# Hybrid attention and HGRN2 layer on one core: value products in one pass of split operands, branch products by mixer on four banks, small zero products at the start

## The chip, the cores and the metric

The kernel runs on one core of one Trainium2 chip. The metric is the device time of one execution in microseconds (us). The engines are TensorE (PE, with its weight loads as PEld), VectorE (DVE), ScalarE (ACT), GpSimd (POOL) and the queue engine SP, which issues most DMAs.

## What is computed

One decoder layer over 512 tokens of 1024 features. Two token mixers read one input projection; their outputs are projected, gated, added, projected again, and a layer norm follows the residual. Cut to what matters:

```python
h = x @ w_in + b_in                   # 5912 columns
# mixer A: 8 heads of 64 in 2 groups; three branches, gated per head
o_cmp = softmax(q k_c^T) v_c          # 31 compressed blocks
o_slc = softmax(q_r k_slc^T) v_slc    # causal (all blocks are chosen at this length)
o_win = softmax(q_r k_win^T) v_win    # causal, window of 512
o_a = (g0*o_cmp + g1*o_slc + g2*o_win) * silu(z_a)
# mixer B: HGRN2, 4 heads of 128, chunks of 64
o_b = rmsnorm(hgrn2(q_b, f_b, i_b)) * norm_g * silu(z_b)
y = sigmoid(gm_a) * (o_a @ w_branch_a) + sigmoid(gm_b) * (o_b @ w_branch_b)
out = layer_norm(2**0.25 * x + y @ w_out)
```

Everything is float32.

## The kernel before, in words

Large products run on split operands: `split2` (L140) writes a ScalarE cast to float32r, the high part, and a VectorE subtraction, the low part. A product of two split operands is three single-pass products (high by high, high by low, low by high). Products that are not split are FP32 products, which the trace shows as two records each.

The order of TensorE, and of its DMAs on SP, is the program's own. `proj` (L239) makes a tile of 128 columns of the input projection: 24 products of 128x512 into one bank of the pool `pa` (two banks). Weight tiles come three tiles ahead, and are split two tiles ahead (`load`, `split`, L186 to L196). Before every six of these products, `weave.tick` (L77) lets chains of small steps go on: mixer B (`hgrn`, L330), its norm (`hgrn_norm`, L408), compressed keys and values, rotary embedding, scores (`attn_scores`, L591) and values (`attn_values`, L633). A chain says by `yield` how many ticks it waits; most numbers are in the table `D` (L64). The other engines take their instructions in the order that the tile scheduler gives them.

`attn_scores` and `attn_values` go by units: a query tile of 128 rows (3, 2, 1, 0) and one branch, or both for tiles 1 and 0. Scores of four heads are made, exponentiated and scaled by gate over sum. `attn_values` then takes one block of 128 keys at a time: for each half `ab` of the heads it transposes four 128x128 tiles of probabilities into a bank of `pst` (two banks), ScalarE copies them (L661), and one FP32 product with the tile `vtok` adds 64 output rows to the bank `po`:

```python
T.matmul(po[64 * ab:64 * ab + 64], vts[j][:, 128 * brs[x] + 64 * ab:128 * brs[x] + 64 * ab + 64],
         pts[ab], start=False, stop=brs[x] == 1 and j == i)
```

Here `vts[j]` is `vtok[:, j]`, the values of 128 keys. The two products of a block are a pair. They are issued after the transposes of the next block, or, for the last block of a unit, two ticks later. The compressed branch starts `po` of each query tile with four FP32 products of 128x128 (`vcB`). ScalarE copies `po` to `asum` (L673); VectorE multiplies with silu(z_a) (L679) and `split2` makes `oa`.

At the start, two zero products (L149) stand ahead of the first real ones, which need the first tiles of x and of the weights. After the last gate tile, `weave.drain()` (L775) finishes the chains. Then, for each of eight column tiles m, 12 products of mixer B and 12 of mixer A go to two `pa` banks; VectorE multiplies each with its gate (L804), adds them (L806), and `split2` makes a piece of y. The output projection (from L821) takes banks of `pa`, `pss` and `pst`. All small tiles come from the pool `t2`, with 69 buffers of 512 columns.

Of the kernel before, what the change touches and what calls it, by code (L numbers as in the profile page):

```python
# [9 lines left out]
F32 = mybir.dt.float32  # L10
# [14 lines left out]
# column groups of w_in  # L25
# [4 lines left out]
# feature tiles after the four of f_b, and the order of the large products  # L30
# [11 lines left out]

def _columns(name):
# [15 lines left out]
# columns of the array of constants  # L59
# [33 lines left out]
def layer_kernel(ctx: ExitStack, tc: tile.TileContext, xT, xn, w0, wi, wg, wf, small, brow, consts,  # L93
# [18 lines left out]
    t2 = ctx.enter_context(tc.tile_pool(name="t2", bufs=69))  # L112
# [23 lines left out]

    def act_set(name):
        return tc.keep_in_program_order(A.preload_act_table_set(name)).ins
# [5 lines left out]
    # ---- start: x, the gates and the four tiles of f_b, one contraction tile at a time  # L144
    A.preload_act_table_set("sigmoid_and_others")
# [11 lines left out]
    for kt in range(KT):  # L157
        xr, wr = T2(), T2()
        dma(xr, xT[:, kt])
        dma(wr, w0[kt])  # L160
# [22 lines left out]
    order = M_TILES + ["br%d" % m for m in range(8)]  # L183
# [38 lines left out]
    vtok = cst.tile([P, 4, 256], F32, name="vtok")  # L222
# [86 lines left out]
    # ---- HGRN2, in steps of two chunks  # L309
# [98 lines left out]
    def hgrn_norm():  # L408
# [20 lines left out]
        for h in range(4):  # L429
# [3 lines left out]
            V.tensor_tensor(o, o, rms[h], ALU.mult)  # L433
            yield 1
# [5 lines left out]
    # ---- compressed keys and values  # L440
# [75 lines left out]
    # ---- rotary embedding and exact two-part operands  # L516
# [36 lines left out]
    # ---- compressed branch: gated probabilities of two tiles' heads, transposed  # L553
# [33 lines left out]
    # ---- selected and window branches, by units of one query tile and one branch (or both)  # L587
# [45 lines left out]
    def attn_values():  # L633
        po = None
        for u, (i, brs) in enumerate(units):
            n, last = 128 * (i + 1), None
            while (u, 1) not in probs or len(PTc) < 2 or len(vts) < 4:
                yield 1
            if brs[0] == 0:
                po = PO()  # L640
                for m in range(4):
                    T.matmul(po[:, 128 * m:128 * m + 128], vcB[:, m], PTc[m // 2][:, 128 * i:128 * i + 128],
                             start=m == 0, stop=False)
                yield D["a1"]

            def products():
                x, j, pts = last
                for ab in range(2):
                    T.matmul(po[64 * ab:64 * ab + 64], vts[j][:, 128 * brs[x] + 64 * ab:128 * brs[x] + 64 * ab + 64],
                             pts[ab], start=False, stop=brs[x] == 1 and j == i)  # L650

            for x in range(len(brs)):
                for j in range(i + 1):
                    pts = []
                    for ab in range(2):
# [4 lines left out]
                        t = T2()  # L660
                        A.copy(t, ps)  # L661
# [10 lines left out]
            if brs[-1] == 1:  # L672
                A.copy(asum[:, :, 128 * i:128 * i + 128], po.rearrange("p (m q) -> p m q", m=4))  # L673
# [12 lines left out]
    # ---- the sequence of large products, the rest woven in  # L686
# [79 lines left out]
    # ---- merge gates: tanh of the half argument  # L766
# [8 lines left out]
    weave.drain()  # L775

    # ---- branch projections and merge; w_out is split alongside
# [9 lines left out]
    y = []  # L787
    load_out(0)
    for m in range(8):
        i = len(M_TILES) + m  # L790
        load(i + 3)
        split(i + 2)
        load_out(m + 1)
        hi, lo = parts[i]
        pp = []
        for s_, o4 in ((1, ob), (0, oa)):
            ps = PA()
            for kt in range(4):
                c = slice(128 * (4 * s_ + kt), 128 * (4 * s_ + kt) + 128)
                T.matmul(ps, hi[:, c], o4[kt][0], start=kt == 0, stop=False)  # L800
                T.matmul(ps, hi[:, c], o4[kt][1], start=False, stop=False)
                T.matmul(ps, lo[:, c], o4[kt][0], start=False, stop=kt == 3)
            r = T2()
            V.scalar_tensor_tensor(r, gm["g%s%d" % ("ab"[s_], m)], 1.0, ps, ALU.add, ALU.mult)  # L804
            pp.append(r)
        V.tensor_tensor(pp[0], pp[0], pp[1], ALU.add)  # L806
        hl = T2(dt=F32R), T2(dt=F32R)
        split2(pp[0], *hl)
        y.append(hl)
        hl = []  # L810
        for hf in range(2):
            hi, lo = T2(dt=F32R), T2(dt=F32R)
            split2(woraw[m][hf], hi, lo)
# [7 lines left out]
    # ---- output projection, residual, layer norm  # L821
# [118 lines left out]
```

## Time and profile before

| | before |
|---|---|
| time, median of 3 runs | 450.17 us (449.98 to 450.28) |
| profiled execution, span from its first to its last instruction | 450.8 us (no other time of its own is listed) |
| TensorE busy | 440.7 us, 98%, 2227 products |
| VectorE busy | 269.2 us, 60% |
| ScalarE busy | 223.3 us, 50% |
| GpSimd busy | 3.3 us |
| TensorE's mean granted clock | 0.996 |
| DMA queues | 47.38 MB, mean 105 GB/s |

Busy time of TensorE includes the pipeline, so that successive matmuls overlap in it: what a product costs is read from the starts of successive products, not from their durations. A row of a time line merges like instructions that follow each other (x4), with the time from the first start to the last end.

### The profile page before, as it was taken

What the parts mean: (1) busy time and instruction counts of PE and PEld (TensorE: products, weight loads), DVE (VectorE), ACT (ScalarE), POOL (GpSimd) and SP (SyncE); (2) the same over time, 40 slices, a digit from 0 to 9 for tenths busy, and PEclk for the clock granted to TensorE, in tenths of its full rate; (3) what the DMA queues carried; (4) which work ended last, traced back from release to release, by engine and by line L of the source; (5) the groups of instructions that cost most, each with busy time, mean ns of one, the idle gap of its engine ahead of it and who ended that gap; (6) DMA issues with size and microseconds to landing.
All of it is one profiled execution on the core that took longest, in us unless ns stands there. A gap on an engine that the chain in (4) does not pass through costs nothing.

```text
span 450.8 us, 6002 instructions
## 1 busy us (share of the span) xinstructions
PE 440.7 (98%) x2227; PEld 351.3 (78%) x2227; DVE 269.2 (60%) x550; ACT 223.3 (50%) x430; POOL 3.3 (1%) x16
## 2 busy tenths in 40 slices
PE   8999999999999999999999999999999999999993
PEld 5778888888898888888767687768767788878883
DVE  5905579994896479966433343445421688865554
ACT  3416543531547254687766556678854345344000
POOL 2000000000000000000000000000000000000000
PEclk9999999999999999999999999999999999999998
DMA  8982700222240544212111122111322452162111
GB/s 271 395 334 79 258 1 0 59 84 70 72 141 23 171 156 160 87 59 95 47 48 47 47 75 67 49 47 48 93 75 113 127 185 110 48 229 84 60 47 47
DMA packets 20444, 47.38 MB, mean 105 GB/s; under 512 B 2880, under 2 KB 3904, under 8 KB 20416
## 3 DMA queue, kind: packets, MB, share of 16 engines
q1 hardware_dynamic: 20416, 47.01, 31.3%
q8 instruction: 17, 0.28, 0.2%
q14 instruction: 11, 0.09, 0.1%
HBM read 41.76 MB, written 2.10 MB: 97 GB/s over the span
## 4 chain that ended last, share of the span: by engine, by line
PE 96%; DVE 2%; DMA 1%; issue 0%; DVEq 0%; SPq 0%
PE pa L101 66%; PE pss L101 15%; PE pso L101 10%; PE pst L105 4%; PE pst L101 1%; DMA t<-in_w_dram 1%; DVE t L455 0%; DVE wlo L142 0%; DVE t L856 0%; DVE t L858 0%; DVE t L804 0%; DVEq L936 0%; DVE t L353 0%; DVE sm_bst L848 0%; DVE t L169 0%
## 5 line engine op out<-in xcount | busy, mean ns | idle before, releaser
L101 PE MATMUL pa<-t,whi 128*128 128x512 f32 x704 | 223.7, 399 | 0.0
L101 PEld LDWEIGHTS pa<-t,whi 128*128 128x128 f32 x704 | 127.3, 188 | 38.2 <-issue 15.0
L101 PE MATMUL pa<-t,wlo 128*128 128x512 f32 x352 | 137.7, 391 | 0.0
L101 PEld LDWEIGHTS pa<-t,wlo 128*128 128x128 f32 x352 | 66.1, 188 | 14.6
L142 DVE TENSOR_TENSOR wlo<-wraw,whi 128x1024 fp32r<-128x1024 f32 x46 | 56.0, 1224 | 28.5 <-ACT whi L141 28.3
L141 ACT CAST whi<-wraw 128x1024 fp32r<-128x1024 f32 x46 | 48.2, 1049 | 42.8 <-PE pa L101 25.6
L614 DVE CUSTOM_DVE_ANT_0 t<-pss,t 128x512 f32<-128x512 f32 (+3 forms) x64 | 30.4, 489 | 58.6 <-PE pss L101 58.4
L101 PE MATMUL pss<-t,t 128*128 128x512 f32 (+5 forms) x296 | 49.4, 321 | 0.4 <-DVE t L361 0.4
L101 PEld LDWEIGHTS pss<-t,t 128*128 128x128 f32 (+1 forms) x296 | 39.2, 175 | 7.2 <-issue 0.7
L101 PE MATMUL pa<-t,t 128*128 128x512 f32 x192 | 44.6, 390 | 0.1
L617 ACT ACTIVATE t<-t,sm_mn 128x512 f32<-128x512 f32 (+3 forms) x64 | 35.8, 561 | 13.4 <-DVE sm_mn L614 13.1
L101 PEld LDWEIGHTS pa<-t,t 128*128 128x128 f32 x192 | 35.9, 188 | 7.9 <-DVE t L804 0.5
L661 ACT COPY t<-pst 128x512 f32<-128x512 f32 x40 | 23.3, 582 | 22.0 <-PE pst L105 21.7
L142 DVE TENSOR_TENSOR t<-t,t 128x512 fp32r<-128x512 f32 x36 | 23.0, 686 | 15.7 <-ACT t L141 15.7
L141 ACT CAST t<-t 128x512 fp32r<-128x512 f32 x36 | 20.4, 622 | 17.9 <-DVE t L806 14.4
L105 PE MATMUL pst<-con,t 128*128 128x128 f32 x185 | 28.1, 273 | 0.0
L105 PEld LDWEIGHTS pst<-con,t 128*128 128x128 f32 x185 | 22.7, 140 | 5.6 <-issue 1.6
L101 PE MATMUL pso<-t,t 128*128 128x128 f32 (+1 forms) x104 | 23.3, 344 | 0.7 <-DVE t L169 0.7
L101 PE MATMUL pso<-t,vtok 128*64 128x512 f32 x80 | 21.6, 618 | 0.0
L101 PEld LDWEIGHTS pso<-t,t 128*128 128x128 f32 x104 | 16.5, 198 | 4.8 <-ACT t L168 1.6
L628 ACT ACTIVATE t<-t,sm_dn 128x512 f32<-128x512 f32 (+3 forms) x32 | 16.3, 559 | 3.6 <-DVE sm_dn L623 3.6
L853 ACT ACTIVATE sm_rs<-sm_ag,epst 128x1 f32<-128x1 f32 x4 | 1.2, 296 | 33.3 <-DVE sm_ag L850 33.3
(144 smaller groups left out, 409.2 us busy)
## 6 DMA issues: line engine op xcount, KB each, us to landing
wraw<-in_wf_dram SPq DMA_DIRECT2D x38, 512.0 KB, 3.5
t<-in_w_dram SPq DMA_DIRECT2D x16, 256.0 KB, 5.9
wraw<-in_wbr_dram SPq DMA_DIRECT2D x8, 512.0 KB, 3.6
t<-in_wout_dram SPq DMA_DIRECT2D x16, 256.0 KB, 3.9
t<-t SPq DMA_DIRECT2D x48, 64.0 KB, 2.0
t<-in_xT_dram SPq DMA_DIRECT2D x8, 256.0 KB, 5.2
t<-in_wi_dram SPq DMA_DIRECT2D x8, 256.0 KB, 7.0
t<-in_xn_dram SPq DMA_DIRECT2D x8, 256.0 KB, 7.5
```

Of the source, the lines that this page charges most:

```text
L101: return tc.keep_in_program_order(nc.tensor.matmul(*a, **k))
L105: return tc.keep_in_program_order(nc.tensor.transpose(*a, **k))
L141: A.copy(dst_hi, src)
L142: V.tensor_tensor(dst_lo, src, dst_hi.bitcast(F32), ALU.subtract)
L614: V.tensor_tensor_reduce(out=p[:, c], in0=ps[:, c], in1=amask[:, 512 - n:512], op0=ALU.add, op1=ALU.min, scale=-0.125, scalar=3.0e38, accu ...
L617: A.activation(p[:, c], p[:, c], AF.Exp, bias=mn[:, k], scale=-1.0, accum_out=den[:, k])
L628: A.mul(ts[m][:, c], ts[m][:, c], den[:, k])
L661: A.copy(t, ps)
L853: A.activation(rs[:, 0:1], ag[:, 1:2], AF.Ln, bias=epst)
```

## The change

- Values: `v` is split into `vv`, in which a block holds, for each branch, 64 columns of high parts of one group, 128 of low parts and 64 of high parts of the other. `vv[..., 0:128]` is then high and low of group 0, and `[128:256]` low and high of group 1. The transposed probabilities are split by `split2` from PSUM. A pair becomes four products of 128x512 with float32r operands into two banks, one for each `ab`; high and low rows are added by VectorE afterwards, and GpSimd adds the sum to `asum`.
- Compressed values: four FP32 products of 128x512, one for each m, ahead of the units, copied to `asum` by ScalarE.
- Branch products: the weight tiles hold two column tiles of one mixer each, in the order `BRANCH` (b0 b2 a0 b4 a2 b6 a4 a6); the products go to `pa` and `pss` in turn, and the chains go on ticking between them, with the drain ahead of a0.
- Start: nine zero products of 128x128, and the first weights are loaded on ScalarE's queue.
- The norm's first product on GpSimd, six numbers in `D`, and 67 instead of 69 buffers in `t2`.

```diff
-D = dict(h0=9, h2=1, h3=6, h4=2, h5=8, h6=2, n0=5, n1=2, n2=10, c0=1, c1=6, c2=7, c3=7,
-         r0=5, p0=6, p1=13, a0=1, a1=3, a2=1, a3=1, a4=1, a5=1, s0=14, s1=21, s2=0, s3=2)
+D = dict(h0=8, h2=4, h3=6, h4=2, h5=8, h6=5, n0=3, n1=2, n2=10, c0=1, c1=6, c2=7, c3=7,
+         r0=5, p0=5, p1=13, a0=1, a1=3, a2=1, a3=1, a4=1, a5=1, s0=14, s1=21, s2=0, s3=2)
...
-    zero = T2()
+    first = T2(), T2()
+    dma_act(first[1], w0[0])
+    act_set("sigmoid_and_others")
+    zero = T2(128)
     V.memset(zero, 0.0)
     warm = PO()
-    for n in (512, 320):
-        T.matmul(warm[:, 0:n], zero[:, 0:128], zero[:, 0:n], start=True, stop=True)
+    for _ in range(9):
+        T.matmul(warm[:, 0:128], zero, zero, start=True, stop=True)
...
-            V.tensor_tensor(vtok[:, tt], ps[:, 0:256], brv, ALU.add)
-            vts.append(vtok[:, tt])
+            v = T2(256)
+            tc.keep_in_program_order(V.tensor_tensor(v, ps[:, 0:256], brv, ALU.add))
+            vd = vv[:, tt].rearrange("p b (g c) -> p b g c", c=64)
+            v4 = v.rearrange("p (b g c) -> p b g c", b=2, c=64)
+            split2(v4, vd[:, :, 0:4:3], vd[:, :, 1:3])
+            vts.append(vv[:, tt])
...
-            V.tensor_tensor(o, o, rms[h], ALU.mult)
-            yield 1
+            G.tensor_tensor(o, o, rms[h], ALU.mult)
+            yield 2
...
     def attn_values():
-        po = None
+        while len(PTc) < 2:
+            yield 1
+        for m in range(4):
+            po = PO()
+            T.matmul(po, vcB[:, m], PTc[m // 2], start=True, stop=True)
+            A.copy(asum[:, m], po)
+            yield 1
...
-                    T.matmul(po[64 * ab:64 * ab + 64], vts[j][:, 128 * brs[x] + 64 * ab:128 * brs[x] + 64 * ab + 64],
-                             pts[ab], start=False, stop=brs[x] == 1 and j == i)
+                    v = vts[j][:, brs[x], 128 * ab:128 * ab + 128]
+                    for k in range(2):
+                        T.matmul(acc[ab], v, pts[ab][k], start=brs[x] == 0 and j == 0 and k == 0,
+                                 stop=brs[x] == 1 and j == i and k == 1)
...
-                        t = T2()
-                        A.copy(t, ps)
+                        t = T2(dt=F32R), T2(dt=F32R)
+                        split2(ps, *t)
...
-                A.copy(asum[:, :, 128 * i:128 * i + 128], po.rearrange("p (m q) -> p m q", m=4))
+                o = T2()
+                for ab in range(2):
+                    own, other = slice(64 * ab, 64 * ab + 64), slice(64 - 64 * ab, 128 - 64 * ab)
+                    A.copy(o[own], acc[ab][other])
+                    V.tensor_tensor(o[own], o[own], acc[ab][own], ALU.add)
+                dst = asum[:, :, 128 * i:128 * i + 128]
+                G.tensor_tensor(dst, dst, o.rearrange("p (m q) -> p m q", m=4), ALU.add)
...
-    weave.drain()
...
+        if mix == "a" and m0 == 0:
+            weave.drain()
+        for m in (m0, m0 + 1):
+            ps = (PA, PS)[m % 2]()
             for kt in range(4):
+                if kt % 2 == 0:
+                    weave.tick()
```

How instructions stand on TensorE at a pair of value products, the first pair of the first unit, before. The names: `pst<-con` is a transpose, `vtok` and `vv` are values, `whi` and `wlo` are the parts of a weight tile.

```order
L105 MATMUL pst<-con,t_1946 128x128
L105 MATMUL pst<-con,t_1965 128x128
L101 MATMUL pso<-t_2052,vtok 64x512
L101 MATMUL pso<-t_2074,vtok 64x512
L101 MATMUL pa<-t_199,whi 128x512
L101 MATMUL pa<-t_200,whi 128x512
```

The same place on TensorE in the changed program.

```order
L108 MATMUL pst<-con,t_1972 128x128
L108 MATMUL pst<-con,t_1987 128x128
L104 MATMUL pso<-t_2095,vv 128x512
L104 MATMUL pso<-t_2096,vv 128x512
L104 MATMUL pso<-t_2124,vv 128x512
L104 MATMUL pso<-t_2125,vv 128x512
L104 MATMUL pa<-t_254,whi 128x512
L104 MATMUL pa<-t_255,whi 128x512
```

Two products of 64 output rows became four of 128, at the same place between the transposes and the large products.

On VectorE, in the same unit, before: `L614` is the maximum of a tile of scores in `pss` (two rows for each), and `wlo` the low part of a weight tile.

```order
L142 TENSOR_TENSOR wlo<-wraw,whi 128x1024
L614 ISA t_2093,sm_mn<-pss,t_304 128x512
L614 ISA sm_mn 128x1
L614 ISA t_2112,sm_mn<-pss,t_304 128x512
L614 ISA sm_mn 128x1
L614 ISA t_2133,sm_mn<-pss,t_304 128x512
```

The same stretch of VectorE in the changed program.

```order
L148 TENSOR_TENSOR wlo<-wraw,whi 128x1024
L148 TENSOR_TENSOR t_2096<-pst,t_2095 128x512
L629 ISA t_2116,sm_mn<-pss,t_311 128x512
L629 ISA sm_mn 128x1
L148 TENSOR_TENSOR t_2125<-pst,t_2124 128x512
L629 ISA t_2137,sm_mn<-pss,t_311 128x512
L629 ISA sm_mn 128x1
L148 TENSOR_TENSOR t_2146<-pst,t_2145 128x512
```

The residuals of the transposed probabilities stand between the maxima, in a queue that is taken in order, behind the weight residual.

TensorE at the passage from the last branch products to the output projection, before: the output tile's first bank is of the pool that the branch products used.

```order
L101 MATMUL pa<-t_3247,whi 128x512
L101 MATMUL pa<-t_3248,whi 128x512
L101 MATMUL pa<-t_3247,wlo 128x512
L101 MATMUL pa<-t_3304,t_3300 128x512
L101 MATMUL pa<-t_3305,t_3300 128x512
```

The same passage in the changed program.

```order
L104 MATMUL pss<-t_3446,whi 128x512
L104 MATMUL pss<-t_3447,whi 128x512
L104 MATMUL pss<-t_3446,wlo 128x512
L104 MATMUL pa<-t_3458,t_3540 128x512
L104 MATMUL pa<-t_3459,t_3540 128x512
```

The last 12 branch products now fill a bank of `pss`; the last `pa` bank was filled 12 products earlier.

## Rows read from the trace of the kernel before

**Rows 1.** The page's chain that ended last, share by engine

```profile
PE 96%; DVE 2%; DMA 1%; issue 0%; DVEq 0%; SPq 0%
```

**Rows 2.** Time line of PE, 220 to 224.5 us: start us, us, instructions

```profile
220.34 0.60 PE L105 MATMUL pst<-con,t 128*128 128x128 f32 x4
220.87 1.08 PE L101 MATMUL pso<-t,vtok 128*64 128x512 f32 x4
221.88 0.73 PE L101 MATMUL pa<-t,whi 128*128 128x512 f32 x2
...
223.84 0.60 PE L105 MATMUL pst<-con,t 128*128 128x128 f32 x4
224.19 0.71 PE L101 MATMUL pa<-t,whi 128*128 128x512 f32 x2
```

**Rows 3.** Time line of PE, 235.5 to 237 us, the end of a unit

```profile
235.58 0.34 PE L101 MATMUL pss<-kl,t 128*128 128x384 f32 x1
235.84 1.08 PE L101 MATMUL pso<-t,vtok 128*64 128x512 f32 x4
236.85 0.66 PE L105 MATMUL pst<-con,t 128*128 128x128 f32 x4
```

**Rows 4.** Time line of PE, 207.5 to 208.5 us, one group of compressed values

```profile
207.55 1.05 PE L101 MATMUL pso<-t,vcB 128*128 128x128 f32 x8
208.35 0.71 PE L101 MATMUL pa<-t,whi 128*128 128x512 f32 x2
```

**Rows 5.** Time line of all engines, 0.9 to 5.4 us

```profile
0.91 0.48 DVE L147 MEMSET t<- 128x512 f32 x1 [0.91 <-PEq L928]
...
1.18 0.42 SPq L108 DMA_DIRECT2D t<-in_w_dram  x1
...
1.45 3.14 PE L101 MATMUL pso<-t 128*128 128x512 f32 x4 [1.45 <-DVE t L147]
...
4.75 0.43 DVE L169 CAST t<-t 128x512 fp32r<-128x512 f32 x1 [3.35 <-DMA t<-in_w_dram]
...
5.32 1.19 PE L101 MATMUL pso<-t,t 128*128 128x512 f32 x2 [0.73 <-DVE t L169]
```

**Rows 6.** Chain of waits by time, 9 to 11 us: start us, us, what

```profile
9.07 0.85 PE pso L101 x2
9.93 0.58 PE pss L101 x2
10.51 0.47 PE pso L101 x2
```

**Rows 7.** Chain of waits by time, 353 to 422 us

```profile
352.92 46.57 PE pa L101 x204
399.51 0.70 DVE t L804
400.25 10.49 PE pa L101 x45
410.75 10.88 PE pss L101 x48
```

**Rows 8.** The page's costliest groups: busy us, mean ns; idle before, releaser

```profile
L142 DVE TENSOR_TENSOR wlo<-wraw,whi 128x1024 fp32r<-128x1024 f32 x46 | 56.0, 1224 | 28.5 <-ACT whi L141 28.3
L141 ACT CAST whi<-wraw 128x1024 fp32r<-128x1024 f32 x46 | 48.2, 1049 | 42.8 <-PE pa L101 25.6 <-issue 12.5 <-DMA wraw<-in_wf_dram 4.6
...
L661 ACT COPY t<-pst 128x512 f32<-128x512 f32 x40 | 23.3, 582 | 22.0 <-PE pst L105 21.7
L142 DVE TENSOR_TENSOR t<-t,t 128x512 fp32r<-128x512 f32 x36 | 23.0, 686 | 15.7 <-ACT t L141 15.7
```

**Rows 9.** Busy time by stretch: A:B, us, busy of PE, PEld, DVE, ACT, POOL

```profile
220.00:352.90 132.90, 132.90 (x660) 95.94 (x658) 48.93 (x160) 83.18 (x197) 0.00 (x0) 1.00 0.21 68
```

**Rows 10.** Groups of POOL by form: busy us, mean ns

```profile
L220 POOL MEMSET t<- 128x512 f32 x4 | 1.9, 526 | 0.0
```

**Rows 11.** Time line of PE, 95 us, in mixer B's chain

```profile
95.17 1.68 PE L101 MATMUL pss<-t,t 128*64 128x64 f32 x16 [0.35 <-DVE t L361]
```

More of the change, by code (lines that the diff above doesn't have):

```diff
@@ L40 @@
 NB = 4 + len(M_TILES)
+BRANCH = [("b", 0), ("b", 2), ("a", 0), ("b", 4), ("a", 2), ("b", 6), ("a", 4), ("a", 6)]
 def _columns(name):
@@ L111, in layer_kernel @@
     strm = ctx.enter_context(tc.tile_pool(name="strm", bufs=3))
-    t2 = ctx.enter_context(tc.tile_pool(name="t2", bufs=69))
+    t2 = ctx.enter_context(tc.tile_pool(name="t2", bufs=67))
     sm = ctx.enter_context(tc.tile_pool(name="sm", bufs=8))
@@ L135, in PO, with dma_act @@
         return pso.tile([P, 512], F32, name="pso", tag="pso")
+    def dma_act(o, i):
+        tc.keep_in_program_order(A.dma_start(o, i))
     def act_set(name):
@@ L142, in split2 @@
         V.tensor_tensor(dst_lo, src, dst_hi.bitcast(F32), ALU.subtract)
-    A.preload_act_table_set("sigmoid_and_others")
-    zero = T2()
+    first = T2(), T2()
+    dma_act(first[1], w0[0])
+    act_set("sigmoid_and_others")
+    zero = T2(128)
     V.memset(zero, 0.0)
     warm = PO()
-    for n in (512, 320):
-        T.matmul(warm[:, 0:n], zero[:, 0:128], zero[:, 0:n], start=True, stop=True)
+    for _ in range(9):
+        T.matmul(warm[:, 0:128], zero, zero, start=True, stop=True)
     sml = cst.tile([P, O_END], F32, name="sml")
@@ L157, in layer_kernel @@
     for kt in range(KT):
-        xr, wr = T2(), T2()
+        xr, wr = first if kt == 0 else (T2(), T2())
         dma(xr, xT[:, kt])
-        dma(wr, w0[kt])
+        if kt:
+            dma(wr, w0[kt])
         if kt == 1:
@@ L180, in layer_kernel @@
                 T.matmul(gps[32 * q:32 * q + 32], wgs[:, 32 * k:32 * k + 32], xs[k], start=k < 4, stop=k >= 4)
-    order = M_TILES + ["br%d" % m for m in range(8)]
+    order = M_TILES + ["br%s%d" % b for b in BRANCH]
     raws, parts = {}, {}
@@ L221, in layer_kernel @@
     kcB = cst.tile([P, 64], F32, name="kcB")
-    vtok = cst.tile([P, 4, 256], F32, name="vtok")
+    vv = cst.tile([P, 4, 2, 256], F32R, name="vv")
     asum = cst.tile([P, 4, 512], F32, name="asum")
@@ L633, in attn_values @@
     def attn_values():
-        po = None
+        while len(PTc) < 2:
[5 more added lines that the diff above has]
+            yield 1
+        acc = None
         for u, (i, brs) in enumerate(units):
             n, last = 128 * (i + 1), None
-            while (u, 1) not in probs or len(PTc) < 2 or len(vts) < 4:
+            while (u, 1) not in probs or len(vts) < 4:
                 yield 1
             if brs[0] == 0:
[L640 to L643, printed above, removed]
+                acc = PO(), PO()
                 yield D["a1"]
@@ L785, in load_out @@
                 dma(woraw[kt][hf], wout[kt, :, 512 * hf:512 * hf + 512])
-    y = []
+    y, rb = [], {}
     load_out(0)
-    for m in range(8):
-        i = len(M_TILES) + m
+    for n, (mix, m0) in enumerate(BRANCH):
+        i = len(M_TILES) + n
         load(i + 3)
         split(i + 2)
-        load_out(m + 1)
+        load_out(n + 1)
         hi, lo = parts[i]
-        pp = []
-        for s_, o4 in ((1, ob), (0, oa)):
-            ps = PA()
+        if mix == "a" and m0 == 0:
+            weave.drain()
+        for m in (m0, m0 + 1):
+            ps = (PA, PS)[m % 2]()
             for kt in range(4):
[L799 to L802, printed above, removed]
-            r = T2()
[L804 to L809, printed above, removed]
+                if kt % 2 == 0:
+                    weave.tick()
+                o4 = (oa if mix == "a" else ob)[kt]
+                c = slice(512 * (m - m0) + 128 * kt, 512 * (m - m0) + 128 * kt + 128)
+                T.matmul(ps, hi[:, c], o4[0], start=kt == 0, stop=False)
+                T.matmul(ps, hi[:, c], o4[1], start=False, stop=False)
+                T.matmul(ps, lo[:, c], o4[0], start=False, stop=kt == 3)
+            r = T2()
+            V.scalar_tensor_tensor(r, gm["g%s%d" % (mix, m)], 1.0, ps, ALU.add, ALU.mult)
+            if mix == "b":
+                rb[m] = r
+            else:
+                V.tensor_tensor(r, r, rb[m], ALU.add)
+                hl = T2(dt=F32R), T2(dt=F32R)
+                split2(r, *hl)
+                y.append(hl)
         hl = []
@@ L812, in layer_kernel @@
             hi, lo = T2(dt=F32R), T2(dt=F32R)
-            split2(woraw[m][hf], hi, lo)
+            split2(woraw[n][hf], hi, lo)
             hl.append((hi, lo))
@@ L920 @@
                    a["w_branch_b"][0]]).reshape(2, 4, 128, 8, 128)
-    wbr = wb.transpose(3, 2, 0, 1, 4).reshape(8, 128, 1024)
+    wbr = np.stack([np.concatenate([wb["ab".index(c), :, :, m + j].transpose(1, 0, 2).reshape(128, 512)
+                                    for j in range(2)], axis=1) for c, m in BRANCH])
     arrays_in = dict(
```

## The prediction

> **What bounds the kernel now.** I read the chain of waits first: TensorE is 96% of what ended last [rows 1], so a change counts only where it shortens TensorE's own row, or makes TensorE wait. Then I read TensorE's time line at the places that the change touches: the values of the selected and window branches between 220 and 353 us [rows 2, 3], the compressed values [rows 4], the start [rows 5, 6] and the passage from the branch products to the output projection [rows 7]. Last come the prices on VectorE and ScalarE and how full these are while the values run [rows 8, 9]. The reader is to see in these rows that TensorE's instructions follow each other without a gap, so that what is saved between them is saved in the end, as long as the other engines still deliver in time.
>
> **The values, the largest term.** There are 40 products with vtok, in 20 pairs (a pair is one block of keys, both halves of the heads). Before, four transposes start at 220.34 and the next large product at 221.88, with a pair between them: 1.54 us. Without a pair, the same four transposes are followed by a large product after 0.35 us (223.84 to 224.19). A pair after transposes thus costs 1.19 us [rows 2]. Of the 20 pairs, 14 stand so; the other 6 close a unit, after other products and before transposes: 1.01 us from their start to the transposes, and the product ahead takes 0.26 us where its 384 columns at 0.228 us per 512 would take 0.17, so 1.10 us [rows 3]. Together 14 x 1.19 + 6 x 1.10 = 23.3 us.
>
> After it there are 80 single-pass products of 128x512. The price of one is that of the large products with split operands: 46.57 us for 204, which is 0.228 us [rows 7]. 80 x 0.228 = 18.3 us. The gain is 5.0 us. The change of mode after the transposes stays, whichever product comes next.
>
> A pair is so cheap now because the two products of one pair fill different halves of the array's columns and run side by side: 4 records take 1.08 us in all, though each product has two records and a record lasts about 0.6 us [rows 2]. The Trainium skill (FP8 and Floating Point Precision, section TensorE Precision Notes) says that true FP32 takes four passes through the array. By that rule alone 40 products would cost 40 x 4 x 0.228 = 36.5 us and the gain would be 18.2 us. The rows above contradict this count for half-height products, and the same skill gives the reason (TensorE: Matmul & The Clock Gate, Part 3, The mechanism): products in different column tiles run concurrently. The change gives this up, since each of its products is full height.
>
> **The compressed values.** Before: four groups, each 8 records, 0.80 us from start to the next large product (207.55 to 208.35) [rows 4]. After: four full-height products of FP32 with 512 columns. None is in the trace at full pace. Below: four single passes, 4 x 0.228 = 0.91 us. Above: the zero products at the start, 3.14 us for 832 columns [rows 5], which is 1.93 us for 512 at half the pace, so 0.97 at the full one, and 0.2 for two changes of mode, 1.17. I take 0.95, since the row of FP32 products of this width is the nearest and holds a first load as well: 4 x 0.15 = 0.6 us lost (0.4 to 1.5).
>
> **The start.** The first real product starts at 5.32, after VectorE's cast of the first weights at 4.75, which waits for a DMA issued at 1.18 [rows 5]. Issued on ScalarE's queue instead, it can start some 0.4 us earlier. But the zero products now have 9 x 128 = 1152 columns instead of 832: 3.14 x 1152/832 = 4.35 us. VectorE fills a quarter of the tile, so they start near 1.15 instead of 1.45, and end near 5.5. The real products thus start about 0.2 us later, with no pause ahead of them, where TensorE stood still for 0.73 us before. TensorE's clock is the gain: two products took 0.85 us up to 9.93 and 0.47 from 10.51 on [rows 6], that is the 1.2 GHz level and then the 2.4 GHz one, which it keeps to the end (the mean granted clock is 0.996). From 5.32 to 10.0 are 4.7 us at half pace. If the full clock comes with the first real products, 2.35 us less 0.2 are gained; if it comes no earlier than before, 0.2 are lost. I take 1.5, since unbroken work now begins 4 us sooner. What the trace shows of it is one rise, after a pause of 0.73 us and 4.7 us of work.
>
> **The passage to the output projection.** The branch products used two banks (pa) in turn, and so does the first output tile. It therefore waits for VectorE's last reading of a bank (399.51 to 400.25). The first 48 output products end at 410.75, that is 11.26 us after 399.49; the next 48 take 10.88 [rows 7]. Between 0.38 and 0.76 us are lost; I take 0.55. With pa and pss in turn, the second pa bank was read one product of 12 earlier, so this wait goes. What is late next there is the last y, which is needed only 42 products later, 9.6 us.
>
> **What is added beside TensorE.** VectorE gets 40 residuals of the transposed probabilities from PSUM, 0.686 us each by the SBUF form [rows 8], 27.4 us on top of 48.9 in a stretch of 132.9 [rows 9]; ScalarE's cast replaces its copy of 0.58 and 8 half copies are added, 83 to 88 us. Neither is full, so the question is lateness. Between the transposes of a pair and its products stand at least 12 large products and the four of the pair before: 16 x 0.228 = 3.6 us of cover. Cast and residual need 0.58 + 0.69 = 1.3. If a weight split (1.05, then 1.22) and another VectorE pass of 0.69 are ahead, it is 1.05 + 1.22 + 0.69 + 0.69 = 3.65, about the cover; with the cast behind as well, 4.2. So bounds of 0 and 20 x 0.6 = 12 us; I take 0.4, since a weight split comes once in 5.5 us only.
>
> The sum of a query tile now ends with two half copies, two VectorE adds, an add on GpSimd, and then the old product with z_a. First A products stand 54 products after the last values, 12.3 us. On VectorE lie 0.58 + 2 x 0.69 + 4 x 0.69 + 2 x 1.22 + 3 x 0.69 = 9.2 us plus the GpSimd add. That has no row: the nearest are GpSimd's memset of the same size, 0.53 us [rows 10], and VectorE's 0.69. Up to 3.1 us it is covered; I take nothing, and above that it costs its excess once. The four GpSimd products in the norm of mixer B can hold VectorE, with weight residuals queued behind; these run two tiles ahead, 48 x 0.228 = 10.9 us of cover. The values' own split (four casts and residuals) lies a hundred products ahead of its use. ScalarE's table load moves behind one DMA issue, long before its first cast.
>
> The other delays in the table D and two fewer buffers in t2 shift mixer B's chain by two to three steps. One wait of TensorE stands there now, 0.35 us for VectorE [rows 11]. It may go, or another may come of the size of a weight residual, 1.2 us. I take 0.
>
> **Sum** against the profiled execution, whose span is 450.8 us (no other time of its own is listed; it is 0.14% over the median of 450.17): -5.0 + 0.6 - 1.5 - 0.55 + 0.4 = -6.05, so 444.75, and 444.1 on the scale of the runs.
>
> **Rivals.**
> - The start gives nothing: the full clock comes as late as before. For it: nothing in the trace shows that zero products bring the clock up, and they end after the weights are there. Against it: the pause that stood ahead of the real products is gone. -5.0 + 0.6 + 0.2 - 0.55 + 0.4 = -4.35, so 445.8. Chance 0.18.
> - Some lateness in one place: an A product waiting for a GpSimd add of 5 us, or a mixer B chain that comes a weight residual late in two places. 2.5 us: 446.6. Chance 0.10.
> - Slower: TensorE waits at the values for the residual, because VectorE takes its work in order and the residual stands behind a weight residual that itself waits for ScalarE. At 0.6 us for each of 20 pairs, 12 us, the time is 444.1 - 0.4 + 12 = 455.7. It decides from 6.45/20 = 0.32 us per pair. Against it: VectorE is idle for 84 of the 132.9 us [rows 9]. Chance 0.07.
> - Much more: every one of the 40 products holds the array for four passes of 0.228 us, and the pairs' short times come of matmul ends that are only modelled. Then 40 x 4 x 0.228 = 36.5 us become 18.3, 13.2 us more than forecast: 430.9. The starts of the products behind the pairs [rows 2, 3] speak against it, and those are not modelled. Chance 0.02.
> - My forecast: 0.63.
>
> **How the numbers follow.** A change of 0.2%, 0.9 us, is about what a measurement of this kernel tells from none. Forecast, first, second and fourth rival are faster, 0.93 together; from that I move 0.05 to no change, for lateness between the second and the third rival, and keep 0.07 for slower. The range: below, all terms at their good ends (values -5.2, compressed +0.4, start -2.15, passage -0.76, mixer B -0.35, no lateness) give -8.1, 442.0; above, no gain at the start and 2 us of lateness give 447.5. 441.8 to 447.5 leaves out the slower rival and the four passes.
>
> **What would show it.** Right: pairs of transposes to next large product with 4 products between them at about 1.27 us; two products at 0.47 us well before 10 us; the first output products in 10.9 us; no idle time of TensorE's weight load put down to VectorE's residual at the values. Wrong: idle time of TensorE before products with vv, put down to VectorE or ScalarE; a granted clock that rises as late as before; TensorE waiting at the first A product.

## The result, and the profile after

The changed kernel takes 445.09 us (444.56 to 445.73, 4 runs), the kernel before 450.23 beside it (449.98 to 452.95, 4 runs): ratio 0.9878, interval 0.9849 to 0.9906. It is 5.1 us faster; forecast were 6.1, to 444.1, with a range of 441.8 to 447.5.

One caution on the spans. Every run lists its span beside its time, and some 1.8 us lie around each span. The profiled execution of before, with its span of 450.8, therefore belongs to a time near 452.6, not to the median: it was one of the rarer longer ones (the list above has one of 452.95). The spans of the two profiles differ by 7.2 us (450.8 and 443.6), the medians by 5.1. The 2 us between them are the start: before's profile came to full pace at 10 us, and its first weight product stands 2.04 us later than after's. The experiments show that most executions of before do not have this.

The chain of the page, after, by engine and then by line (the first of its two lines answers to [rows 1]):

```profile
PE 90%; DVE 2%; SPq 2%; ACT 2%; DMA 2%; issue 1%; POOL 0%; DVEq 0%; POOLq 0%; ACTq 0%
PE pa L104 56%; PE pss L104 19%; PE pso L104 10%; PE pst L108 5%; SPq L111 2%; PE pst L104 1%; DMA wraw<-in_wf_dram 1%; ACT whi L147 1%; DVE wlo L148 1%; DMA t<-t 0%; POOL t L448 0%; ACT t L564 0%; DVE t L891 0%; DVE t L893 0%; DVE t L450 0%
```

TensorE's share of the chain fell from 96% to 90%: the chain now passes through a wait in mixer B, through SP's queue and the norm. TensorE is still busy for 434.1 of 443.6 us, so this share says little about what bounds the kernel.

**Values.** TensorE's time line after, a pair of value products behind transposes, and the same transposes without a pair (start us, us, instructions), as in [rows 2]:

```profile
223.91 0.60 PE L108 MATMUL pst<-con,t 128*128 128x128 f32 x4
224.27 1.18 PE L104 MATMUL pso<-t,vv 128*128 128x512 f32 x4
225.28 0.62 PE L104 MATMUL pa<-t,whi 128*128 128x512 f32 x2
225.75 0.40 PE L104 MATMUL pa<-t,wlo 128*128 128x512 f32 x1
...
227.12 0.60 PE L108 MATMUL pst<-con,t 128*128 128x128 f32 x4
227.48 0.71 PE L104 MATMUL pa<-t,whi 128*128 128x512 f32 x2
```

TensorE's time line before, the row that follows the pair of [rows 2]:

```profile
222.45 0.40 PE L101 MATMUL pa<-t,wlo 128*128 128x512 f32 x1
```

From the first transpose to the next large product it was 1.54 us and is 1.37. The pair itself takes 1.01 us from start to start both times (220.87 to 221.88, 224.27 to 225.28); what is saved stands on its two sides. It starts 0.36 us after the first transpose, where it started after 0.53. And the two large products behind it take 0.47 us (225.28 to 225.75), where they took 0.57: the first of them 0.235 from its start to the next one's, before 0.335. So a pair costs 0.27 us less (0.17 and 0.10), in all 14 places. TensorE's time line after, the end of a unit as in [rows 3]:

```profile
237.85 0.33 PE L104 MATMUL pss<-kl,t 128*128 128x384 f32 x1
238.02 1.09 PE L104 MATMUL pso<-t,vv 128*128 128x512 f32 x4
238.95 0.60 PE L108 MATMUL pst<-con,t 128*128 128x128 f32 x4
```

At the 6 ends of units the pair takes 0.92 or 0.93 instead of 1.01 us, and its neighbours on both sides take some 0.1 less each (the one ahead 0.17 here, 0.26 in [rows 3]): 1.6 us for the six. Together 14 x 0.27 + 1.6 = 5.4 us. No value product shows idle time. The prediction called such a dearer neighbour a change of mode; the traces show its time, not what it is made of.

The compressed values, TensorE's time line after (compare [rows 4]):

```profile
201.67 1.02 PE L104 MATMUL pso<-t,vcB 128*128 128x512 f32 x2
202.13 1.03 PE L104 MATMUL pa<-t,whi 128*128 128x512 f32 x2
203.00 0.39 PE L104 MATMUL pa<-t,wlo 128*128 128x512 f32 x1
```

TensorE's time line before, the row that follows [rows 4]:

```profile
208.90 0.39 PE L101 MATMUL pa<-t,wlo 128*128 128x512 f32 x1
```

After, the next large product starts 0.455 us after the FP32 product, but takes 0.63 itself instead of 0.23: 0.859 us in all. Before, a group took 0.808 and the product behind it 0.085 too long (0.55 for two, 208.35 to 208.90, where two take 0.46): 0.893, and 1.0 in the last unit. The four groups save 0.25 us. 0.859/4 is 0.215 us, near one pass of 512 columns: for a full-height product the trace agrees with the four passes that the Trainium skill names (FP8 and Floating Point Precision, section TensorE Precision Notes).

The groups of splits on VectorE and ScalarE (busy us, mean ns; idle before), new beside [rows 8]:

```profile
L148 DVE TENSOR_TENSOR t<-pst,t 128x512 fp32r<-128x512 f32 x40 | 27.5, 689 | 15.7 <-ACT t L147 15.7
L147 ACT CAST t<-pst 128x512 fp32r<-128x512 f32 x40 | 23.1, 580 | 17.6 <-PE pst L108 17.5
```

The residual from PSUM takes 0.689 us, as assumed from the SBUF form.

**Start.** TensorE's time line after, against [rows 5, 6]:

```profile
1.05 4.21 PE L104 MATMUL pso<-t 128*128 128x128 f32 x18 [1.05 <-DVE t L156]
5.28 0.95 PE L104 MATMUL pso<-t,t 128*128 128x512 f32 x2
6.07 0.63 PE L104 MATMUL pss<-t,t 128*128 128x512 f32 x2
6.53 0.61 PE L104 MATMUL pso<-t,t 128*128 128x512 f32 x2
```

The real products start at 5.28 (5.32 before) without a pause, and from 6.07 on two take 0.46 us from start to start. In the profile of before that pace came at 10. The pace is what to read here: in before the granted clock of 5.3 to 10 us reads 1.00, while its products take 0.427 us.

**Passage to the output projection.** The chain of waits after, in order of time:

```profile
392.70 10.88 PE pa L104 x48
403.58 10.88 PE pss L104 x48
```

No VectorE step stands in it, and the first 48 products take what the others take; in [rows 7] it was 11.26. The wait itself is 0.4 of the 0.46 us gained here.

**A new wait.** The chain of waits after, in mixer B:

```profile
62.65 0.45 PE pst L108 x4
63.10 0.02 issue
63.12 0.70 DVE t L275
63.83 0.04 issue
63.87 2.31 PE pa L104 x9
```

The VectorE add of the first i tile starts only when the four transposes of the gates end, and TensorE waits for its bank: 0.78 us idle. Another small one stands at 171.5 (0.36 us), and the one of [rows 11] is gone. Between the first weight product (2.04 us ahead of before) and the first score product (0.89 ahead) 1.15 us are lost.

**Where it went.** From the first score product to the start of the output projection after gains 5.9 us, in the first 48 products of the projection 0.4. In usual executions: 5.8 (values, compressed values and small rests) + 0.46 (passage) - 1.15 (mixer B) + 0 (start) = 5.1, the measured difference.

### The profile page after: what moved, and what is told of

It reads as the page before. It is cut to its first block, busy times and chain, and to the rows that moved or that the text cites. A ratio compares the mean times of both kernels' runs of the same rounds, so it can differ in the third digit from the quotient of the medians.

```text
span 443.6 us, 6069 instructions
## 1 busy us (share of the span) xinstructions
PE 434.1 (98%) x2217; PEld 361.5 (81%) x2217; DVE 299.6 (68%) x598; ACT 228.2 (51%) x442; POOL 13.6 (3%) x24
## 4 chain that ended last, share of the span: by engine, by line
PE 90%; DVE 2%; SPq 2%; ACT 2%; DMA 2%; issue 1%; POOL 0%; DVEq 0%; POOLq 0%; ACTq 0%
PE pa L104 56%; PE pss L104 19%; PE pso L104 10%; PE pst L108 5%; SPq L111 2%; PE pst L104 1%; DMA wraw<-in_wf_dram 1%; ACT whi L147 1%; DVE wlo L148 1%; DMA t<-t 0%; POOL t L448 0%; ACT t L564 0%; DVE t L891 0%; DVE t L893 0%; DVE t L450 0%
## 5 line engine op out<-in xcount | busy, mean ns | idle before, releaser
L104 PE MATMUL pa<-t,whi 128*128 128x512 f32 x640 | 203.5, 399 | 0.0
L104 PEld LDWEIGHTS pa<-t,whi 128*128 128x128 f32 x640 | 116.8, 188 | 25.9 <-issue 3.9
L104 PE MATMUL pa<-t,wlo 128*128 128x512 f32 x320 | 125.2, 391 | 0.0
L104 PEld LDWEIGHTS pa<-t,wlo 128*128 128x128 f32 x320 | 60.1, 188 | 13.3
L104 PE MATMUL pss<-t,t 128*128 128x512 f32 (+5 forms) x296 | 48.4, 318 | 0.0
L148 DVE TENSOR_TENSOR t<-pst,t 128x512 fp32r<-128x512 f32 x40 | 27.5, 689 | 15.7 <-ACT t L147 15.7
L147 ACT CAST t<-pst 128x512 fp32r<-128x512 f32 x40 | 23.1, 580 | 17.6 <-PE pst L108 17.5
L104 PE MATMUL pso<-t,vv 128*128 128x512 f32 x80 | 22.9, 408 | 0.0
L104 PE MATMUL pso<-t,t 128*128 128x128 f32 (+1 forms) x104 | 22.1, 332 | 0.0
L104 PE MATMUL pss<-t,whi 128*128 128x512 f32 x64 | 19.7, 389 | 0.0
```

The costliest lines, as they stand in the source:

```text
L104: return tc.keep_in_program_order(nc.tensor.matmul(*a, **k))
L147: A.copy(dst_hi, src)
L148: V.tensor_tensor(dst_lo, src, dst_hi.bitcast(F32), ALU.subtract)
```

## The experiments

All times are medians of the runs, and ratios are to runs of before on the same chip. The chips differ (e5 to e8 ran on another one than the other experiments), so experiments are compared by their ratios.

**The start alone, on before** (e1_start)

```diff
+    dma_act(first[1], w0[0])
...
-    for n in (512, 320):
+    for _ in range(9):
```

> The kernel before with the start alone changed (first weights on ScalarE's queue, nine zero products of 128x128). Theory A, as predicted: the full clock comes earlier in every execution, 1.5 to 2.0 us faster than the kernel before, ratio 0.9956 to 0.9967. Rival B: the profiled execution of the kernel before was one in which the clock rose late (10.0 us), and in most of its executions it rises near the first real product; then the median moves by 0.0 to 0.5 us only, ratio 0.999 to 1.000, while this kernel's own profile shows two products at 0.47 us by 6.1 us.

Measured: 450.26 us (12 runs, 450.06 to 451.05) against 450.39 (23 runs); ratio 0.9992, 0.998 to 1.0005. The start gives nothing to the median that these runs can tell from no change; the 1.5 us forecast lie outside the interval.

**The values alone, on before** (e2_values)

```diff
-    vtok = cst.tile([P, 4, 256], F32, name="vtok")
+    vv = cst.tile([P, 4, 2, 256], F32R, name="vv")
...
-                        A.copy(t, ps)
+                        split2(ps, *t)
```

> The kernel before with the values alone changed (split operands, sums on GpSimd, compressed values in four wide products, 67 buffers), with the old start, old table D and old branch products. Theory A: the arithmetic of TensorE's starts holds, 4.4 us faster (5.0 gained on the pairs, up to 0.6 lost on the compressed values), ratio about 0.990. Rival: VectorE's 40 residuals come late without the other delays, at least 0.1 us lost for each pair, 2 us or less gained, ratio 0.9955 or more. As the last A products now wait for more steps without the two B tiles ahead, A expects up to 3 us of wait at the first A product, which would bring the ratio to 0.997.

Measured: 456.67 us, ratio 1.0153 (1.0119 to 1.0187): slower than before. TensorE's time line, at the end of mixer B and at the first branch products, shows why:

```profile
148.68 0.39 PE L101 MATMUL pa<-t,wlo 128*128 128x512 f32 x1
152.64 1.14 PE L101 MATMUL pa<-t,whi 128*128 128x512 f32 x2 [3.57 <-DVE t L285]
153.57 0.63 PE L101 MATMUL pa<-t,wlo 128*128 128x512 f32 x1
...
356.75 0.39 PE L101 MATMUL pa<-t,wlo 128*128 128x512 f32 x1
359.75 0.51 PE L101 MATMUL pa<-t,whi 128*128 128x512 f32 x1 [2.61 <-ACT t L141]
360.90 0.79 PE L101 MATMUL pa<-t,whi 128*128 128x512 f32 x1 [0.65 <-DVE t L142]
```

VectorE's time line at the first wait:

```profile
149.03 0.69 DVE L438 TENSOR_TENSOR t<-t,t 128x512 f32<-128x512 f32 x1 [0.38 <-DMA t<-t]
151.47 0.69 DVE L438 TENSOR_TENSOR t<-t,t 128x512 f32<-128x512 f32 x1 [1.74 <-DMA t<-t]
152.07 0.42 DVE L285 TENSOR_TENSOR t<-pa,t 128x256 f32<-128x256 f32 x1
```

A norm product (L438) waits in VectorE's row for its DMA; the add that frees TensorE's bank (L285) stands behind it in the same row. The second wait is the first A products, which wait for the sums of the last query tile. And after each wait TensorE runs at half pace. Busy time by stretch (PE, PEld, DVE, ACT, POOL, granted clock, DMA share, GB/s):

```profile
144.00:148.60 4.60, 4.60 (x22) 3.81 (x21) 2.40 (x2) 3.37 (x4) 0.00 (x0) 1.00 0.24 57
152.64:156.13 3.49, 3.49 (x9) 2.72 (x9) 2.38 (x4) 0.88 (x2) 0.00 (x0) 0.51 0.46 107
156.40:160.00 3.60, 3.60 (x17) 2.96 (x16) 0.92 (x2) 1.06 (x2) 0.00 (x0) 1.00 0.97 337
```

The granted clock is 0.51 for 3.49 us behind the wait, the 1.2 GHz level, and 1.00 on both sides. Lost are 3.7 + 1.7 us at the first place and 3.7 + 1.7 at the second (two waits together), and 1.1 up to there in mixer B, 0.83 of it at 62.7 us, where after waits too; the values give 5.8 back. That is 6.1 of the 6.3 measured.

**The branch products alone, on before** (e3_branch)

```diff
-            ps = PA()
+            ps = (PA, PS)[m % 2]()
```

> The kernel before with the branch products alone changed (one mixer for each weight tile, banks of pa and pss in turn, drain ahead of the first A tile). Theory A: only the wait at the output projection goes, 0.4 to 0.7 us faster, ratio 0.9984 to 0.9991. Rival: the four banks bring nothing that shows, ratio 1.000, because the next wait there takes its place.

Measured: 450.26 us (12 runs), ratio 1.0000, 0.9985 to 1.0015. In the trace the wait at the passage is gone (0.47 us), too little for the runs to show. With the old start its products came to full pace at 6.8 us.

**After with the old start** (e4_oldstart)

```diff
-    dma_act(first[1], w0[0])
...
-    for _ in range(9):
+    for n in (512, 320):
```

> The changed kernel with the old start (two zero products, first weights on SP's queue). Theory A, as predicted: 1.5 to 2.0 us slower than the changed kernel, so about 3.3 us faster than the kernel before, ratio 0.9926. Rival B (the old start raises the clock early in most executions): within 0.5 us of the changed kernel, ratio 0.988 to 0.989.

Measured: 444.80 us, ratio 0.9875 (0.9855 to 0.9896), the same as after. The full pace came at 4.8 us. TensorE's time line:

```profile
4.93 0.70 PE L104 MATMUL pso<-t,t 128*128 128x512 f32 x2 [0.34 <-DVE t L172]
5.47 0.62 PE L104 MATMUL pss<-t,t 128*128 128x512 f32 x2
```

In the other traces with the old start it came at 5.9 (e2) and 6.8 us (e3). So the old start too brings the clock up early, and before's profile, with 10.0, was an exception.

What the new start may do is remove these: of 68 runs with the old start in before, e3 and e4, 12 lay at 452.05 to 452.95 where the kernel's median was 450.2 to 450.8; of 12 runs of e1 none lay above 451.05, and no other kernel with the nine zero products and no long wait had a run 1.1 us above its median (37 more). That is a count over different kernels, and only one such run has a trace, so it is a lead and not shown.

**After with the old table D, and the norm's product on VectorE** (e5_oldsched)

```diff
-D = dict(h0=8, h2=4, h3=6, h4=2, h5=8, h6=5, n0=3, n1=2, n2=10, ...
+D = dict(h0=9, h2=1, h3=6, h4=2, h5=8, h6=2, n0=5, n1=2, n2=10, ...
...
-            G.tensor_tensor(o, o, rms[h], ALU.mult)
-            yield 2
+            V.tensor_tensor(o, o, rms[h], ALU.mult)
+            yield 1
```

> The changed kernel with the old delays in table D and the norm's first product on VectorE again. Theory A (from the values alone): the norm's product on VectorE waits for its DMA with the add of the value tile behind it, so that TensorE waits some 4 us for a pa bank near 149 us and then works at half pace for some 3.4 us: 5 to 6 us slower than the changed kernel, about 450.5, ratio 1.000. Rival B: the wait there belongs to the values alone in the old order of the branch stage and is gone here: 445, ratio 0.988.

Measured: 455.61 us, ratio 1.0097 (1.0071 to 1.0124), worse than expected. The wait of e2 is there (3.98 us at 149.8, start to start), another of 2.7 at 368.9, at an A product, and half pace for 3.4 us behind each. TensorE's time line:

```profile
153.76 1.04 PE L104 MATMUL pa<-t,whi 128*128 128x512 f32 x2 [3.59 <-DVE t L295]
...
371.60 0.50 PE L104 MATMUL pa<-t,whi 128*128 128x512 f32 x1 [2.18 <-DVE t L148]
```

The second wait was not expected; together the two and their half pace are 9.6 of the 9.9 us by which the kernel is slower than after.

**After with the norm's product on VectorE, new table** (e11_normdve)

```diff
-            G.tensor_tensor(o, o, rms[h], ALU.mult)
+            V.tensor_tensor(o, o, rms[h], ALU.mult)
```

> The changed kernel with the norm's first product on VectorE instead of GpSimd, and the new delays in D. Theory A: the move to GpSimd is what takes the wait for the DMA of the norm out of VectorE's queue, so TensorE waits some 4 us near 150 us again and works at half pace after it: 4 to 6 us slower than the changed kernel, ratio 0.998 to 1.002. Rival B: the delays in D are what does it, and the product's engine is free: within 0.7 us of the changed kernel, ratio 0.987 to 0.990.

Measured: 445.06 us, ratio 0.9873 (0.9848 to 0.9897): no difference to after, so here the engine of this product does not matter. With e5, what takes the long waits away is the new delays in D, or the `yield 2` behind the product, which this kernel keeps and e5 does not. Which of them, and which of the five changed entries of D (five, not six), was not tried; nor were the old delays with the product on GpSimd.

**After with the old branch products** (e6_nobranch)

```diff
-BRANCH = [("b", 0), ("b", 2), ("a", 0), ("b", 4), ("a", 2), ("b", 6), ("a", 4), ("a", 6)]
...
-            ps = (PA, PS)[m % 2]()
+            ps = PA()
```

> The changed kernel with the old branch products (12 B and 12 A products for each weight tile, two banks, drain ahead of all of them). Theory A: the first A products come some 12 products after the last B products instead of 48, the chain from the last values over the GpSimd add to oa takes 9 to 10 us, TensorE waits about 3.0 us and then works at half pace for some 3.4 us, and the old wait of 0.45 us at the output projection is back: 4.5 to 5.5 us slower than the changed kernel, about 450, ratio 0.999. Rival B: the sums arrive in time and only the 0.45 us come back: 445.5, ratio 0.989.

Measured: 449.1 us, ratio 0.9958 (0.9942 to 0.9973), 3.6 us slower than after by the ratios. TensorE's time line at the first A products, which here stand 18 products behind the values' end instead of 54:

```profile
351.57 0.50 PE L101 MATMUL pa<-t,whi 128*128 128x512 f32 x1 [0.31 <-ACT t L144]
352.72 0.50 PE L101 MATMUL pa<-t,whi 128*128 128x512 f32 x1 [0.65 <-DVE t L145]
...
353.93 0.50 PE L101 MATMUL pa<-t,whi 128*128 128x512 f32 x1 [0.24 <-DVE t L145]
...
355.66 0.50 PE L101 MATMUL pa<-t,whi 128*128 128x512 f32 x1 [0.78 <-DVE t L145]
```

Four waits, 2.75 us from start to start beyond the products' own time, and none is followed by the half pace that had been expected. With the dearer products behind the waits the branch products take 3.4 us longer than after's (48.29 against 44.89), and the old wait of 0.4 us at the output projection is back. On the kernel before, the new order gave nothing that the runs show (e3); behind the new values it is worth 3.6 us: it is the cover of their tail.

**The gates' chain two row tiles earlier** (e7_gates)

```diff
-        if t == 2:
+        if t == 0:
             weave.start(gates())
```

> The changed kernel with the chain of the branch gates started two value tiles earlier, so that the buffer of the raw gates is free before the first tile of i is added. Theory A: the wait of 0.8 us at 63 us, where VectorE's add of the first tile of i waits for that buffer with 67 in the pool, goes: 0.6 to 0.9 us faster than the changed kernel, ratio 0.986. Rival B: mixer B's chain starts from the same adds and the time returns as a wait near 90 us: no change, ratio 0.988.

Measured: 444.10 us (443.8 to 444.28), ratio 0.9848 (0.9825 to 0.987). The wait at 63 us is gone. The gain is 1.0 us by the medians and 1.4 by the ratios; the intervals overlap, but all four runs lie below all of after's (444.56 to 445.73), and from the first weight product to the first score product the trace takes 156.85 us, where after takes 158.34 and before 157.19. This agrees with the cause that the trace suggests: the raw gates hold buffers of t2 until their transposes, and the add of the first i tile needs one. e2, with 67 buffers and the old table D, has this wait as well; before, with 69 and the same table, has not, and up to that place what the two programs do differs in nothing but the number of buffers. After with 69 buffers was not run.

**The norm's row DMAs two at a time** (e8_spread)

```diff
+                if b % 2:
+                    yield 1
-        yield D["n2"]
+        yield D["n2"] - 8
```

> The changed kernel with the 16 row DMAs of the norm issued two for each tick instead of all at once, so that weight loads can pass between them on SP's queue (issue of the 16 took 11.2 us, 146.75 to 158). Theory A: the load of the weight tile needed at 171 us comes earlier and the wait of 0.36 us at 171 goes: 0.3 to 0.5 us faster than the changed kernel, ratio 0.987. Rival B: the norm comes later and the time goes elsewhere: no change, 0.988.

Measured: 444.73 us, ratio 0.9865 (0.9841 to 0.9888): not told apart from after. The wait at 171 us is absent here, but also in e4 and e7, which leave the DMAs as they were; it does not come in every trace, and what the edit does to it stays open.

**The residual of the transposed probabilities made twice** (e9_double)

```diff
                         split2(ps, *t)
+                        V.tensor_tensor(t[1], ps, t[0].bitcast(F32), ALU.subtract)
```

> The changed kernel with the residual of the transposed probabilities made twice on VectorE (40 more passes of 0.69 us, 27.5 us). Theory A: the residuals have cover and VectorE is not near its limit between 220 and 350 us, so TensorE waits little: 0 to 1 us slower than the changed kernel, ratio 0.988 to 0.990. Rival (the slower one of the prediction): VectorE's order is already at the edge of its cover, and each further 0.69 us delays a pair: 40 x 0.69 less nothing gives up to 27 us, and anything over 6.5 us makes it slower than the kernel before.

Measured: 445.39 us, ratio 0.9877 (0.9852 to 0.9902). Forty more VectorE passes of 0.69 us, and the only new wait in TensorE's time line is the first one:

```profile
221.21 0.39 PE L104 MATMUL pss<-kl,t 128*128 128x512 f32 x1
221.97 0.63 PE L108 MATMUL pst<-con,t 128*128 128x128 f32 x4 [0.37 <-DVE t L686]
```

The runs show no loss against after. The cover of the residuals is wide; the slower rival had no ground.

**One zero product instead of nine** (e10_nozero)

```diff
-    for _ in range(9):
+    for _ in range(1):
```

> The changed kernel with one zero product of 128x128 instead of nine. Theory A: zero products bring the clock up as real ones do, which is why both starts came up early in most executions; without them the full clock comes near 10 us and the time is 2 to 2.5 us longer than that of the changed kernel, ratio 0.993. Rival: zero products do not count, and the clock comes up as before: no change, ratio 0.988.

Measured: 446.73 us, ratio 0.9905 (0.9881 to 0.993), 1.2 us slower than after by the ratios, where 2 to 2.5 were expected. The intervals overlap, but all six runs (446.31 to 447.39) lie above all of after's (444.56 to 445.73). TensorE's time line:

```profile
1.05 0.80 PE L104 MATMUL pso<-t 128*128 128x128 f32 x2 [1.05 <-DVE t L156]
5.08 1.19 PE L104 MATMUL pso<-t,t 128*128 128x512 f32 x2 [3.24 <-ACT t L178]
...
9.48 0.98 PE L104 MATMUL pss<-t,t 128*128 128x512 f32 x2
10.30 0.64 PE L104 MATMUL pso<-t,t 128*128 128x512 f32 x2
```

The full pace comes at 10.2, as in [rows 6], and the first weight product at 31.7 instead of 29.7. So the trace and the runs agree that zero products bring the clock up; the old start had enough of them already in most executions.

**After with both schedule edits and the third compressed product in a pss bank** (e12_best)

```diff
+                if b % 2:
+                    yield 1
-        yield D["n2"]
+        yield D["n2"] - 8
...
-            ps = PT()
+            ps = (PT, PS)[g]()
...
-        if t == 2:
+        if t == 0:
```

> The changed kernel with the three small waits of TensorE taken away: gates two value tiles earlier (0.8 us at 63 us), the row DMAs of the norm spread (0.36 us at 171 us, not in every execution), and the third product of the compressed keys and values in a bank of pss instead of pst (0.5 us at 137 us). Theory A: all are on TensorE's row and nothing replaces them, 1.2 to 1.7 us faster than the changed kernel, ratio 0.9845, the fastest of all here. Rival B: the third one only moves the wait to the next user of a pss bank: 0.8 us faster, as with the gates alone.

Measured: 443.32 us (443.08 to 443.99), ratio 0.9832 (0.9808 to 0.9856): the lowest median of all. It is 2.1 us faster than after by the ratios and 1.8 by the medians, more than the 1.2 to 1.7 expected, and all its runs lie below all of after's; it is not told apart from the gates alone (e7) by the intervals. The waits at 63, 137 and 171 us are all absent.

## Why the prediction was right, and where its steps were not

The time came out 1.0 us above the forecast and inside the range. The largest term held. The start and mixer B came out 2.65 us worse than forecast, the values, the compressed values and the lateness 1.65 better, so that it landed within 1.0 us is in part luck.

- **Values, "the gain is 5.0 us": right, 5.4.** 0.28 us a pair was forecast behind transposes and 0.27 is there; at the six ends it was 0.19, and 0.27 came. The sign "about 1.27 us" did not come, it was 1.37: the missing 0.10 appears behind the pair, in the next large product. The four products take 0.92 us at the ends, as forecast, but 1.01 behind transposes, as the old pair did; there the gain stands in what the pair costs the products beside it. The rival of four passes for each old product is refuted: it had asked for a gain of 18.2.
- **Compressed values, "0.6 us lost": mis-sized.** 0.95 us for one product against 0.80 was the step. Measured are 0.859 against 0.893 to 1.0, with the slow products behind both counted: 0.25 gained. I had left that neighbour out for the old groups.
- **Lateness, "I take 0.4": none**, and with the residuals doubled (e9) one wait of 0.37 us. The slower rival is refuted.
- **The start, "I take 1.5": failed for the median.** The step read one rise of the clock, at 10 us, as the kernel's usual one. e2, e3 and e4 show it at 5.9, 6.8 and 4.8 with the old start, and e1 gives nothing that its runs tell from no change. What speaks for the step, that zero products bring the clock up, agrees with e10. This is the rival "the start gives nothing", though for another reason than it gave. The same rare execution was the base of the sum: its span was taken as 0.14% over the median, when 1.8 us lie around each span; 450.17 less the 6.05 gives 444.1 as well, so the forecast was not moved by that.
- **Passage, "I take 0.55": right, 0.46 in the trace.** In the runs it is too small to show (e3).
- **Mixer B's delays and two fewer buffers, "I take 0": failed.** 1.15 us are lost there, about 1 us of it at the add that waits for the gates' transposes (e7); the runs point to the two buffers taken away. So the second rival, one place late by a couple of us, also came about, at half its price, in a place that the text named only in general.
- **What the prediction did not price:** the new D (with the `yield` beside it) and the order of the branch products look like edits worth 0 and 0.55, and are the condition of the rest. With the old D and the norm's product as it was (e5) the kernel is 9.9 us slower by the ratios, without the order 3.6 (e6). The text had the danger of products in the norm holding VectorE, but put it on the weight residuals, with 10.9 us of cover; behind them stands the value add, which frees a bank and has no such cover (e2).
- **The tail of the sums** had about the length that was said: 11 us from the last value product to the last part of `oa` (347.6 to 358.7), where 9.2 and the GpSimd add had been said. That add took 1.30 us, inside the 3.1 of cover, and no A product waits. GpSimd's and VectorE's time lines after, of the last sum:

```profile
349.48 1.30 POOL L703 TENSOR_TENSOR asum<-asum,t 128x512 f32<-128x512 f32 x1 [13.31 <-DVE t L701]
```

```profile
350.81 0.69 DVE L709 TENSOR_TENSOR asum<-asum,t 128x512 f32<-128x512 f32 x1 [1.41 <-POOL asum L703]
```

The sum with the measured terms: -5.4 - 0.25 - 0.15 (rest of that stretch) - 0.46 + 1.15 + 0 = -5.1.

## What to carry to other kernels

Price a product together with its neighbours: here a product of split operands took 0.10 us longer behind transposes or half-height FP32 products, and 0.40 longer behind a full-height FP32 product. Check which execution a profile caught before a stretch of it becomes a term: one profile with a late clock cost this forecast 1.5 us. And where a part of a change looks idle in the profile of before, ask what it covers in the other parts; two such parts were worth 3.6 and 9.9 us here. Of the 9.9, 3.4 are the half pace that followed two waits of TensorE of 3.75 and 2.4 us; the short waits of the 3.6 had none.

## What the runs showed of the hardware

- Waits of TensorE of 3.75 and 2.4 us in e5, of 3.7 us in e2 and of 2.8 and 0.9 us close together in e2 were each followed by about 3.4 us at half the granted clock (0.51 where the table above has it), with products of 0.427 us instead of 0.228. Four waits of 0.4 to 0.9 us within 5 us (e6) were not.
- Products of zeros ahead of the real ones went with an earlier full pace: 10.2 us with one of them (e10), 5.8 in after's profile with nine, one trace each; the runs of the two differ by 1.2 us by the ratios. The time differs between executions and kernels alike, from 4.8 to 7.2 in the traces with the old or the new zeros, and 10.0 in the one of before.
- GpSimd's add of two 128x512 FP32 tiles took 1.26 to 1.30 us, VectorE's 0.69.
